# Stage changes of a two-model kernel: weight chunks split ahead of each norm, and a new order of work around them

## The chip, the cores and the metric

One core of one Trainium2 chip. The metric is the device time of one execution in microseconds, the median of several runs. The kernel before took 2974.73 us (three runs, 2971.39 to 2978.29).

## What is computed

Two small transformers run one after the other on 256 tokens of width 1024 (`D`), everything in float32. The first has a short convolution, a SwiGLU, a dilated attention and a mixture of eight experts; the second takes the first one's output and a context of 256 more tokens through a mixer of mLSTM and gated linear attention, a convolutional feed-forward, an RWKV-7 mixer and another such feed-forward. Every one of these layers is wrapped in the same way, and the change is about that wrapping:

```
def modulated_residual(x, c, g, w_mod, b_mod, fn):
    shift, scale, gate = ada_params(c, w_mod, b_mod)
    h = rms_norm(x, g) * (1 + scale) + shift
    return x + gate * fn(h)          # fn begins with h @ W

hl = modulate(rmsnorm(xl, norm_g[layer, 0]), mod_l[0], mod_l[1])   # second model, latent
hc = modulate(rmsnorm(xc, norm_g[layer, 0]), mod_c[0], mod_c[1])   # second model, context
v  = (hn + (shift(hn) - hn) * mu[3]) @ w_rkv[2]                    # RWKV values, both sequences
```

## The kernel before

Activations are kept transposed, eight blocks (`KT`) of 128 channels, each 256 tokens wide; the second model keeps both sequences side by side in `xj`, sequence 0 the context, 1 the latent. A product in float32 precision is made of three matmuls: each operand is split into a high part (`hi`, rounded by ScalarE) and a low part (`lo`, the rest, by VectorE), and TensorE adds hi·hi, hi·lo and lo·hi. `wchunk` (L239) does it for weights: SyncE loads a chunk of 512 KB into `raw`, ScalarE writes `whi` (L254), VectorE `wlo` (L255). There are three pairs of `whi`/`wlo`, so that a chunk can be split only when the one three before it has been used.

Each call of `wchunk` also gives credit to a background job (`background`, L151), which loads modulation weights for a later layer; `mods_v` sums them on VectorE into `macc` (L211, L213).

Where one layer ends and the next begins, the order is always this. The last products are added into `x`; ScalarE squares, TensorE sums the squares over partitions (L331), ScalarE takes Ln and Exp to get the inverse root; then for each block VectorE multiplies (`nt`), ScalarE adds the shift and rounds (`hh`), VectorE makes the low part (`hl`). That is `modulated` (L359) for one sequence and `modulated2` (L917) for two. The first matmul of the next layer needs the first `hh`, the first `whi`, and soon `hl` and `wlo`.

Six stage changes are touched:

- into the SwiGLU (layer 0), about 150 us from the start; into the attention (`layer1_attn`), about 356 us, where after the norm the positions are loaded (L500) and cast by VectorE (L502) for the rotary tables;
- out of the experts into the second model's first mixer, about 1370 us. `first_norms` (L1411) makes the first model's final norm and the second model's first norm from one pass of squares, then calls `modulated2` for both sequences, then scales `x` eight times (L1441). Then come the mixer's masks (`masks0`, L882), then `even_mixer` (L972) with the narrow gate weights (raw loads L981, split L300 and L301, 24 matmuls L990) and the wide ones (L293);
- into the feed-forward `conv_ffn2`, about 1715 us, with background jobs for the next layer at 48 steps over 66 chunks;
- into the RWKV projections (`rwkv_project`, L1524), about 2112 us: `mix(3)` (L1551) norms, shifts and mixes all eight blocks, then the value product (L1590) runs over two halves of 512 output columns (`c`), and inside over pairs of blocks (`k0`), with four banks of PSUM;
- into the last feed-forward `conv_ffn1`, about 2747 us.

Each engine and each queue works its instructions strictly in the order in which they were put there when the program was built. That order isn't the order of the program text: a planner with a timing model of its own walks along, and whenever an engine is free in its model it takes, of the instructions that the model holds ready, the one that stands first in the text. Moving a call ahead in the text therefore gives it precedence and does not of itself make it run earlier.

Of the kernel before, what the change touches and what calls it, by code (L numbers as in the profile page):

```python
# [14 lines left out]
P = 128  # L15
# [17 lines left out]
def _body(es, tc, A, out, upto, dbg):  # L33
# [106 lines left out]
    back.update(jobs=[], rate=0.0, credit=0.0)  # L140
# [10 lines left out]
    def background(jobs, chunks):  # L151

        back["jobs"] += [g for _, g in jobs]
        back["rate"] = sum(n for n, _ in jobs) / chunks
        back["credit"] = 0.0
# [285 lines left out]
    def layer0():  # L441
# [39 lines left out]
        a01 = scale_col("a01", NG(0, 1), m01[:, 8:16])  # L481
        hh, hl = modulated(fb, x, a01, m01[:, 0:8], st=st.rstd())
# [7 lines left out]
    def layer1_attn():  # L490
# [5 lines left out]
        a10 = scale_col("a10", NG(1, 0), m10[:, 8:16])  # L496
        hh, hl = modulated(fb, x, a10, m10[:, 0:8], st=M.get("rs"))
# [384 lines left out]
    def masks0(pl):  # L882
# [17 lines left out]
        nc.vector.memset(reset, 1.0)  # L900
        rv = reset.rearrange("p z (c u) -> p z c u", u=64)
        nc.vector.memset(rv[:, 0, :, 0:1], 0.0)
        nc.vector.memset(rv[:, 1, :, 63:64], 0.0)
# [68 lines left out]
    def even_mixer(pl, xs, y):  # L972

        W = A["ev_w_in_2"][0]
        ML_CN, ML_M0, GL_S = H0["CN"], H0["M0"], H0["S"]

# [5 lines left out]
        whi = whl.tile([P, 1024], F32R, name="whi")  # L982
        wlo = whl.tile([P, 1024], F32R, name="wlo")
        split(raw[:, :896], whi[:, :896], wlo[:, :896])
        hi, lo = (t[:, :896].rearrange("p (k n) -> p k n", k=8) for t in (whi, wlo))
# [22 lines left out]
        with ExitStack() as st:  # L1008
# [402 lines left out]
    def first_norms(pl, xj, cols):  # L1411

        x = xj[:, :, 1]
        if "fin" not in stages:
            return modulated2(pl, xj, cols, seqs(rstd2(xj)))
# [3 lines left out]
        nc.vector.tensor_tensor(ga, fg, cols[1][0], op=MULT)  # L1419

        pt = ps.tile([P, 512], F32, name="st")
# [20 lines left out]
        return xs  # L1442

    def layer2_0(xj):
# [16 lines left out]
        with phase("m0", dict(mm=4, tr=2, sc=2, st="sc"), t2=5), ExitStack() as st:  # L1461
# [6 lines left out]
            even_mixer(pl, xs, y)  # L1468
# [52 lines left out]
    def rwkv_project(pr, pl, xj, cols):  # L1521
# [29 lines left out]
        def mix(i, both=True, first=False):  # L1551
# [3 lines left out]
            for k in range(KT):  # L1555
# [24 lines left out]
        xs = mix(3, first=True)  # L1580
        V = o["V"] = pr.tile([P, 2, 2, D], F32, name="V")
        for c in range(2):
            pts = [ps.tile([P, 512], F32, name="mm") for _ in range(4)]
            for k0 in range(0, KT, 2):
                hi, lo = wchunk(rkv[2][k0 * P:(k0 + 2) * P, c * 512:(c + 1) * 512].rearrange("(k p) n -> p k n", p=P), [2, 512])
                for i in range(4):
                    for k in range(2):
                        xh, xl = (t[:, i * P:(i + 1) * P] for t in xs[k0 + k])
                        for j, (w, x_) in enumerate(((hi, xh), (hi, xl), (lo, xh))):
                            nc.tensor.matmul(pts[i], x_, w[:, k], start=(k0 + k + j == 0), stop=(k0 + k == 7 and j == 2))  # L1590
            for i in range(4):
                nc.scalar.activation(V[:, i // 2, i % 2, c * 512:(c + 1) * 512], pts[i], AF.Copy)
# [636 lines left out]
    def layer2_1(xj):  # L2229
# [108 lines left out]
```

## Time and profile before

| what | value |
|---|---|
| median of three runs | 2974.73 us (2971.39 to 2978.29) |
| the profiled execution, own time | 2965.52 us |
| its span, first to last instruction | 2963.7 us |
| TensorE busy | 2795.3 us, 94% |
| VectorE busy | 2270.0 us, 77% |
| ScalarE busy | 1700.2 us, 57% |
| mean granted TensorE clock | 0.970 of full |

The profiled execution was 9.2 us shorter than the median of the runs. Busy time of TensorE counts pipelined matmuls, and tells little of whether a stretch is full; the table by stretches of time, the order of instructions on an engine (timeline) with the idle time ahead of each and what ended it, and the chain of waits tell more. In this profile the chain that ended last can be followed back to about 1390 us only; the start of the execution has to be read from timelines.

### The profile page before, as it was taken

The numbers are of one execution on the slowest core, as the hardware profiler recorded it, in microseconds if no ns is written. First come the engines' busy times: TensorE is split into PE (matmuls) and PEld (weight loads), VectorE is DVE, ScalarE is ACT, GpSimd is POOL, SyncE is SP. The second block draws the span as 40 slices with busy tenths as digits, with TensorE's granted clock in tenths as the row PEclk, the third lists the DMA queues.
The fourth block names the chain that finished last, engine by engine and source line by source line (L and its number), as shares of the span: only waits on it lengthen the run. The fifth ranks groups of instructions, "written<-read, shape, count | busy, mean of one in ns | idle before, by whom it ended". The sixth has DMA issues, their size and how long they took to land.

```text
span 2963.7 us, 50177 instructions
## 1 busy us (share of the span) xinstructions
PE 2795.3 (94%) x19215; PEld 2269.2 (77%) x19237; DVE 2270.0 (77%) x3945; ACT 1700.2 (57%) x2897; POOL 16.8 (1%) x96
## 2 busy tenths in 40 slices
PE   7999899899999999997999889999699999999998
PEld 4999876688777877875867668888477777667998
DVE  3999673799898988987666498768767887675886
ACT  3565443677777877875455444333457677564454
POOL 0000000000000000000000000000000000000000
PEclk9999999999999999998999999999899999999999
DMA  9989677799898998994311235554222111113463
GB/s 320 325 285 348 226 220 250 269 349 355 295 376 329 328 338 331 356 318 142 93 36 51 79 105 180 169 172 143 81 76 48 29 30 20 18 27 110 130 185 122
DMA packets 410412, 567.73 MB, mean 192 GB/s; under 512 B 79719, under 2 KB 241715, under 8 KB 410163
## 3 DMA queue, kind: packets, MB, share of 16 engines
q1 hardware_dynamic: 406976, 561.79, 56.0%
q8 instruction: 153, 2.51, 0.3%
q10 hardware_dynamic: 3187, 2.65, 0.3%
q14 instruction: 96, 0.79, 0.1%
HBM read 559.11 MB, written 5.24 MB: 190 GB/s over the span
## 4 chain that ended last, share of the span: by engine, by line
PE 41%; DVE 7%; ACT 3%; DMA 1%; issue 1%; SPq 0%; ACTq 0%; DVEq 0%
PE mm L293 20%; PE mm L958 2%; PE yp L1389 2%; PE mm L1590 1%; PE kc L1697 1%; PE tr L1957 1%; PE p L2014 1%; PE p L1993 1%; PE p L2037 1%; PE mm L1855 1%; PE p L2026 1%; PE mm L1878 1%; PE tr L1944 1%; PE sc L1271 1%; PE tr L1575 0%
## 5 line engine op out<-in xcount | busy, mean ns | idle before, releaser
L254 ACT ACTIVATE whi<-raw 128x1024 fp32r<-128x1024 f32 (+3 forms) x868 | 875.8, 1019 | 597.9 <-PE mm L293 164.8
L255 DVE TENSOR_TENSOR wlo<-raw,whi 128x1024 fp32r<-128x1024 f32 (+3 forms) x868 | 1002.7, 1171 | 196.8 <-ACT whi L254 169.1
L795 PE MATMUL mm<-wlo,XH 128*128 128x512 f32 (+1 forms) x768 | 289.3, 379 | 6.6 <-DVE wlo L255 6.1
L795 PE MATMUL mm<-whi,XL 128*128 128x512 f32 (+1 forms) x768 | 289.9, 378 | 0.0
L293 PE MATMUL mm<-hh,whi 128*128 128x512 f32 (+1 forms) x800 | 280.1, 352 | 10.1 <-DVE fg L1341 3.2
L795 PE MATMUL mm<-whi,XH 128*128 128x512 f32 (+1 forms) x768 | 287.8, 375 | 0.2 <-ACT whi L254 0.2
L293 PE MATMUL mm<-hh,wlo 128*128 128x512 f32 (+1 forms) x800 | 278.0, 348 | 4.6 <-DVE wlo L255 4.6
L293 PE MATMUL mm<-hl,whi 128*128 128x512 f32 (+1 forms) x800 | 278.4, 349 | 0.0
L213 DVE SCALAR_TENSOR_TENSOR macc<-raw,sc,macc 128x512 f32<-128x512 f32 x238 | 175.7, 747 | 30.0 <-DMA raw<-in_w_mod_dram 26.5
L293 PEld LDWEIGHTS mm<-hh,whi 128*128 128x128 f32 x800 | 154.9, 194 | 30.8 <-issue 4.7
L795 PEld LDWEIGHTS mm<-wlo,XH 128*128 128x128 f32 x768 | 145.5, 189 | 36.2 <-DVE wlo L255 10.8
L293 PEld LDWEIGHTS mm<-hh,wlo 128*128 128x128 f32 x800 | 154.5, 193 | 24.0 <-DVE wlo L255 5.0
L293 PEld LDWEIGHTS mm<-hl,whi 128*128 128x128 f32 x800 | 154.6, 193 | 18.7 <-issue 1.0
L795 PEld LDWEIGHTS mm<-whi,XH 128*128 128x128 f32 x768 | 145.5, 190 | 24.5 <-ACT whi L254 0.6
L795 PEld LDWEIGHTS mm<-whi,XL 128*128 128x128 f32 x768 | 145.3, 189 | 24.6
L271 PE MATMUL mm<-hh,whi 128*128 128x256 f32 x544 | 153.7, 283 | 3.9 <-ACT hh L368 3.9
L271 PE MATMUL mm<-hl,whi 128*128 128x256 f32 x544 | 153.1, 282 | 0.2 <-DVE hl L372 0.2
L271 PE MATMUL mm<-hh,wlo 128*128 128x256 f32 x544 | 152.7, 281 | 0.0
L1341 DVE SCALAR_TENSOR_TENSOR fg<-mm,c_fcw,fg 128x189 f32<-128x189 f32 (+2 forms) x352 | 143.9, 426 | 4.6
L813 PE MATMUL mm<-whi,muh 128*128 128x512 f32 x352 | 138.2, 393 | 0.1
L813 PE MATMUL mm<-whi,mul 128*128 128x512 f32 x352 | 137.2, 390 | 0.0
L813 PE MATMUL mm<-wlo,muh 128*128 128x512 f32 x352 | 117.3, 393 | 0.2
(700 smaller groups left out, 5890.1 us busy)
## 6 DMA issues: line engine op xcount, KB each, us to landing
raw<-in_moe_w_down_dram SPq DMA_DIRECT2D x176, 512.0 KB, 7.3
raw<-in_moe_w_gate_dram SPq DMA_DIRECT2D x160, 512.0 KB, 5.2
raw<-in_moe_w_up_dram SPq DMA_DIRECT2D x160, 512.0 KB, 5.4
raw<-in_ffn_w_up_dram SPq DMA_DIRECT2D x110, 512.0 KB, 4.6
raw<-in_mod_w_dram SPq DMA_DIRECT2D x96, 512.0 KB, 5.8
raw<-in_w_mod_dram SPq DMA_DIRECT2D x96, 512.0 KB, 4.5
raw<-in_ffn_w_down_dram SPq DMA_DIRECT2D x62, 512.0 KB, 4.4
raw<-in_ev_w_in_dram SPq DMA_DIRECT2D x28, 512.0 KB, 3.7
```

Of the source, the lines that this page charges most:

```text
L213: nc.vector.scalar_tensor_tensor(acc, w[:, kk], v[:, k + kk:k + kk + 1], acc, op0=OP.mult, op1=OP.add)
L254: nc.scalar.activation(hi[:, :n], raw[:, :n], AF.Copy)
L255: nc.vector.tensor_tensor(lo[:, :n], raw[:, :n], R(hi[:, :n]), op=OP.subtract)
L271: nc.tensor.matmul(pt[:, b], w[:, k, b * P:(b + 1) * P], x[:, k0 + k], start=(k0 + k + b == 0 and j == 0), stop=(k0 + k == kt - 1 and j == ...
L293: nc.tensor.matmul(pts[b], w[:, k, b * P:(b + 1) * P], x_, start=(k0 + k + j == 0 and (b == 0 or N != T)), stop=(k0 + k == kt - 1 and j == ...
L795: nc.tensor.matmul(pt[:, :n], xx[:, k0 + k, i], w[:, k], start=(k0 + k == 0 and j == 0), stop=(k0 + k == 7 and j == 2))
L813: nc.tensor.matmul(py[q], xx[:, k0 + k], w[:, k, q * 512:(q + 1) * 512], start=(k0 + k == 0 and j == 0), stop=(k0 + k == FB - 1 and j == 2))
L958: nc.tensor.matmul(pts[i][:, :n], x_, w[:, k], start=(k0 + k + j == 0), stop=(k0 + k == 7 and j == 2))
L1271: nc.tensor.matmul(o, l, r, start=(n == 0), stop=(n == len(jobs) - 1), skip_group_check=True)
L1341: nc.vector.scalar_tensor_tensor(d4[:, ro, co], s4[:, ri, cin], tap(dy, dx), d4[:, ro, co], op0=MULT, op1=ADD)
L1389: nc.tensor.matmul(yk[k], w[:, 0, k * P:(k + 1) * P], u, start=(f + b + j == 0 and k % 2 == 0), stop=(f + b == FB - 1 and j == 2 and k % 2 ...
L1590: nc.tensor.matmul(pts[i], x_, w[:, k], start=(k0 + k + j == 0), stop=(k0 + k == 7 and j == 2))
```

## The change

`ready` and `ready4` call `wchunk` for the first two chunks of the next layer ahead of the norm's code and put the split pairs on a list; the next two calls of `wchunk` take them from there. They are called ahead of the SwiGLU, the attention, both convolutional feed-forwards and the RWKV values. Into the second model's first mixer the narrow weights are loaded and split inside `first_norms`; the context's eight products come ahead of the final norm's end, the blocks are then written sequence by sequence, and the scaling of `x` and the masks move behind the mixer's value product. The background jobs of `conv_ffn2` start after ten chunks and then go faster. RWKV's values are mixed two blocks at a time, each pair followed by its share of the product for both halves of the columns, in eight banks of PSUM. Some `memset`s go from VectorE to GpSimd, and a small tile that nobody reads shifts the addresses of the last stage's tiles.

```diff
-    def background(jobs, chunks):
+    def background(jobs, chunks, wait=0):
         back["jobs"] += [g for _, g in jobs]
-        back["rate"] = sum(n for n, _ in jobs) / chunks
-        back["credit"] = 0.0
+        back["rate"] = sum(n for n, _ in jobs) / (chunks - wait)
+        back["credit"] = -wait * back["rate"]
...
     def wchunk(ap, shape):
+        if back["ready"]:
+            return back["ready"].pop(0)
...
+    def ready(*aps):
+        back["ready"] = [wchunk(a.rearrange("(k p) n -> p k n", p=P), [a.shape[0] // P, a.shape[1]]) for a in aps]
+    def ready4(W):
+        ready(W[0:512, 0:256], W[512:1024, 0:256])
...
+        ready4(A["ffn_w_gate"][0])
         hh, hl = modulated(fb, x, a01, m01[:, 0:8], st=st.rstd())
...
+        ready(A["attn_w_qkv"][0][0:256, 0:512], A["attn_w_qkv"][0][256:512, 0:512])
         hh, hl = modulated(fb, x, a10, m10[:, 0:8], st=M.get("rs"))
...
         reset = pl.tile([P, 2, 2 * T], F32, name="reset")
-        nc.vector.memset(reset, 1.0)
+        nc.gpsimd.memset(reset, 1.0)
...
-    def even_mixer(pl, xs, y):
+    def narrow_weights():
         raw = wraw.tile([P, 1024], F32, name="raw")
         nc.gpsimd.memset(raw[:, :896], 0.0)
...
+        def finish():
+            split(raw[:, :896], whi[:, :896], wlo[:, :896])
+        return finish
...
             gemmT(W, 1024, 512, xs, v_emit)
+            later()
             for s in range(2):
                 mlstm(pm, s, qk, vx, IF, y)
...
+        def product(s, k, a, rs):
+            t = ts[k] if s == 0 else tmp.tile([P, T], F32, name="nt", bufs=2)
+            nc.vector.scalar_tensor_tensor(t, xj[:, k, s], a[:, k:k + 1], rs, op0=MULT, op1=MULT)
+            return t
+        def high(s, k, t):
+            nc.scalar.activation(ops[k][0][:, s], t, AF.Identity, bias=cols[s][1][:, k:k + 1])
+        def low(s, k, t):
+            nc.vector.scalar_tensor_tensor(ops[k][1][:, s], t, cols[s][1][:, k:k + 1], R(ops[k][0][:, s]), op0=ADD, op1=SUB)
...
+        for k in range(KT):
+            product(0, k, cols[0][0], rsb[:, 0])
         cp = tmp.tile([P, 2 * T], F32, name="sq2", tag="t2", bufs=sizes["t2"])
         nc.scalar.activation(cp, pt, AF.Copy)
...
+        got = between()
+        for k in range(3):
+            high(0, k, ts[k])
...
         nc.scalar.activation(fr, fr, AF.Exp, scale=-0.5)
-        xs = modulated2(pl, xj, [cols[0], (ga, cols[1][1])], [rsb[:, 0], fr[:, 1]])
-        for k in range(KT):
-            nc.vector.scalar_tensor_tensor(x[:, k], x[:, k], fg[:, k:k + 1], fr[:, 0], op0=MULT, op1=MULT)
+        for k in range(3):
+            low(0, k, ts[k])
+        for k in range(KT + 1):
+            if k < KT:
+                t = product(1, k, ga, fr[:, 1])
+                high(1, k, t)
+                if k >= 3:
+                    high(0, k, ts[k])
+            if last is not None:
+                low(1, k - 1, last)
+            if 3 <= k < KT:
+                low(0, k, ts[k])
+            last = t
+        def scale():
+            for k in range(KT):
+                nc.vector.scalar_tensor_tensor(x[:, k], x[:, k], fg[:, k:k + 1], fr[:, 0], op0=MULT, op1=MULT)
...
-            xs = first_norms(pl, xj, both("a20", 0, 0))
-            masks0(pl)
+            xs, scale, narrow = first_norms(pl, xj, both("a20", 0, 0), narrow_weights())
+            def later():
+                scale()
+                masks0(pl)
...
-                background([j0, j1], 66)
+                background([j0, j1], 66, 10)
+            ready4(A["ffn_w_up_2"][0])
             xs = modulated2(pl, xj, both("a21", 2, 3), rs)
...
-        xs = mix(3, first=True)
+        ready(rkv[2][0:256, 0:512], rkv[2][0:256, 512:1024])
+        xs = []
-        for c in range(2):
-            pts = [ps.tile([P, 512], F32, name="mm") for _ in range(4)]
-            for k0 in range(0, KT, 2):
+        pts = [ps.tile([P, 512], F32, name="tr" if i < 2 else "mm") for i in range(8)]
+        for k0 in range(0, KT, 2):
+            xs += mix(3, first=True, ks=(k0, k0 + 1))
+            for c in range(2):
                 hi, lo = wchunk(rkv[2][k0 * P:(k0 + 2) * P, c * 512:(c + 1) * 512]...)
...
+            pl.tile([P, 48], F32, name="beside")
+            ready4(A["ffn_w_up_2"][1])
             hh, hl = modulated(pl, x, scale_col("a31", NG2(1, 2), m(4)), m(3), bufs=2, st=M["rsr"])
```

## Rows read from the trace of the kernel before

**Rows 1.** The page's first part: busy us, share of the span, instructions.
```profile
PE 2795.3 (94%) x19215; PEld 2269.2 (77%) x19237; DVE 2270.0 (77%) x3945; ACT 1700.2 (57%) x2897; POOL 16.8 (1%) x96
```
**Rows 2.** ScalarE's timeline into the SwiGLU: start, us, operation, idle before and releaser.
```profile
147.73 1.06 ACT L254 ACTIVATE whi<-raw 128x1024 fp32r<-128x1024 f32 x1 [2.19 <-PE mm L271]
```
**Rows 3.** Timeline of ScalarE, then VectorE, into the attention.
```profile
356.10 1.04 ACT L254 ACTIVATE whi<-raw 128x1024 fp32r<-128x1024 f32 x1
357.04 1.29 ACT L368 ACTIVATE hh<-nt,mod_m 128x256 fp32r<-128x256 f32 x3
...
356.22 1.28 DVE L367 SCALAR_TENSOR_TENSOR nt<-xj,a,rs 128x256 f32<-128x256 f32 x3 [1.44 <-ACT rs L349]
...
363.04 0.17 DVE L502 CAST pos<-pos_i 128x2 f32<-128x2 int32 x1 [5.27 <-DMA pos_i<-in_positions_dram]
...
364.27 0.88 DVE L372 SCALAR_TENSOR_TENSOR hl<-nt,mod_m,hh 128x256 fp32r<-128x256 f32 x2
```
**Rows 4.** Stretches into the attention: us, busy by engine, granted clock, DMA share, GB/s.
```profile
365.00:370.00 5.00, 5.00 (x14) 3.75 (x14) 5.00 (x16) 4.07 (x7) 0.00 (x0) 0.61 1.05 397
370.00:375.00 5.00, 4.81 (x20) 2.95 (x20) 5.00 (x11) 1.82 (x3) 0.00 (x0) 1.00 0.83 280
```
**Rows 5.** Chain of waits out of the experts: start, us, piece.
```profile
1394.68 1.01 DVE wlo L301
...
1395.74 7.16 PE tr L990 x22
```
**Rows 6.** TensorE's timeline there.
```profile
1383.26 0.77 PE L990 MATMUL tr<-hh,whi 128*112 128x512 f32 x1 [4.88 <-ACT hh L927]
...
1396.30 0.63 PE L990 MATMUL tr<-hh,whi 128*112 128x512 f32 x1
1396.73 0.63 PE L990 MATMUL tr<-hl,whi 128*112 128x512 f32 x1
```
**Rows 7.** Timelines of VectorE (two lines) and ScalarE (one) there.
```profile
1382.31 1.54 DVE L926 SCALAR_TENSOR_TENSOR nt<-xj,fga,frs 128x256 f32<-128x256 f32 x4
...
1391.29 3.24 DVE L1441 SCALAR_TENSOR_TENSOR xj<-xj,c_a,frs 128x256 f32<-128x256 f32 x8
...
1380.20 0.93 ACT L300 ACTIVATE whi<-raw 128x896 fp32r<-128x896 f32 x1
```
**Rows 8.** Chain of waits in the first feed-forward of the second model.
```profile
1745.12 1.15 DVE wlo L255
...
1746.31 7.19 PE mm L293 x20
...
1782.49 32.66 PE mm L293 x144
```
**Rows 9.** TensorE's timeline at that point.
```profile
1746.31 0.80 PE L293 MATMUL mm<-hh,wlo 128*128 128x512 f32 x1 [4.57 <-DVE wlo L255]
```
**Rows 10.** The background sums (macc) alone, by stretches there: us, VectorE busy.
```profile
1717.00:1742.00 25.00, 5.47 (x8) 0.93 0.20 64
1742.00:1754.00 12.00, 3.54 (x7) 0.72 0.57 172
```
**Rows 11.** All engines over the RWKV mixing: us, PE, PEld, DVE, ACT, POOL, clock.
```profile
2111.00:2139.00 28.00, 10.57 (x28) 7.33 (x27) 25.34 (x52) 16.31 (x30) 0.00 (x0) 0.63 0.52 170
2111.00:2177.00 66.00, 48.57 (x196) 38.79 (x195) 51.58 (x91) 31.10 (x52) 0.00 (x0) 0.84 0.35 108
2177.00:2199.00 22.00, 19.10 (x74) 13.20 (x73) 20.46 (x47) 13.48 (x25) 2.61 (x13) 0.83 0.00 0
```
**Rows 12.** Chain of waits into the RWKV projections.
```profile
2110.55 7.00 DMA raw<-in_rw_w_rkv_dram
...
2132.90 43.92 PE mm L1590 x184
```
**Rows 13.** Timelines there: TensorE's first matmul, then ScalarE.
```profile
2119.20 1.22 PE L1590 MATMUL mm<-whi,mh 128*128 128x512 f32 x2 [7.51 <-ACT mh L300]
...
2113.63 2.10 ACT L1534 ACTIVATE hf<-hf,mod_b1a 128x256 f32<-128x256 f32 x5 [0.55 <-DVE hf L1533]
```

More of the change, by code (lines that the diff above doesn't have):

```diff
@@ L137, in _body @@
     nc.vector.tensor_scalar(msel, mi, 0.0, None, op0=OP.is_equal)
-    back.update(jobs=[], rate=0.0, credit=0.0)
+    back.update(jobs=[], rate=0.0, credit=0.0, ready=[])
     def back_step():
@@ L899, in masks0 @@
         reset = pl.tile([P, 2, 2 * T], F32, name="reset")
-        nc.vector.memset(reset, 1.0)
+        nc.gpsimd.memset(reset, 1.0)
         rv = reset.rearrange("p z (c u) -> p z c u", u=64)
-        nc.vector.memset(rv[:, 0, :, 0:1], 0.0)
-        nc.vector.memset(rv[:, 1, :, 63:64], 0.0)
+        nc.gpsimd.memset(rv[:, 0, :, 0:1], 0.0)
+        nc.gpsimd.memset(rv[:, 1, :, 63:64], 0.0)
         mdir = pl.tile([8, 2], F32, name="mdir")
@@ L970, in _body @@
     f2 = lambda t: t.rearrange("p s t -> p (s t)")
-    def even_mixer(pl, xs, y):
+    def narrow_weights():
         W = A["ev_w_in_2"][0]
-        ML_CN, ML_M0, GL_S = H0["CN"], H0["M0"], H0["S"]
         raw = wraw.tile([P, 1024], F32, name="raw")
@@ L981, in even_mixer @@
             nc.sync.dma_start(rv[:, :, r:r + n], W[:, c:c + n].rearrange("(k p) n -> p k n", p=P))
[L982 to L985, printed above, removed]
+        def finish():
+            whi = whl.tile([P, 1024], F32R, name="whi")
+            wlo = whl.tile([P, 1024], F32R, name="wlo")
+            split(raw[:, :896], whi[:, :896], wlo[:, :896])
+            return tuple(t[:, :896].rearrange("p (k n) -> p k n", k=8) for t in (whi, wlo))
+        return finish
+    def even_mixer(pl, xs, y, narrow, later):
+        W = A["ev_w_in_2"][0]
+        ML_CN, ML_M0, GL_S = H0["CN"], H0["M0"], H0["S"]
+        hi, lo = narrow
         pt = ps.tile([P, 512], F32, name="tr")
@@ L1409, in conv_ffn1, with first_norms @@
         return yk, st.rstd()
-    def first_norms(pl, xj, cols):
+    def first_norms(pl, xj, cols, between):
         x = xj[:, :, 1]
         if "fin" not in stages:
-            return modulated2(pl, xj, cols, seqs(rstd2(xj)))
+            return modulated2(pl, xj, cols, seqs(rstd2(xj))), lambda: None, between()
         fg = C1["final_g"]
@@ L1419, in first_norms @@
         nc.vector.tensor_tensor(ga, fg, cols[1][0], op=MULT)
+        ops = [tuple(pl.tile([P, 2, T], F32R, name=n, bufs=8) for n in ("hh", "hl")) for _ in range(KT)]
+        def product(s, k, a, rs):
[6 more added lines that the diff above has]
+            nc.vector.scalar_tensor_tensor(ops[k][1][:, s], t, cols[s][1][:, k:k + 1], R(ops[k][0][:, s]), op0=ADD, op1=SUB)
+        st_ = ExitStack()
+        pt_ = st_.enter_context(tc.tile_pool(reuse_waits="tile", name="fn", bufs=1))
+        POOLS.append(pt_)
+        ts = [pt_.tile([P, T], F32, name="ct", bufs=KT) for _ in range(KT)]
         pt = ps.tile([P, 512], F32, name="st")
@@ L1438, in first_norms @@
         nc.scalar.activation(fr, fr, AF.Exp, scale=-0.5)
-        xs = modulated2(pl, xj, [cols[0], (ga, cols[1][1])], [rsb[:, 0], fr[:, 1]])
-        for k in range(KT):
-            nc.vector.scalar_tensor_tensor(x[:, k], x[:, k], fg[:, k:k + 1], fr[:, 0], op0=MULT, op1=MULT)
-        return xs
+        for k in range(3):
+            low(0, k, ts[k])
+        last = None
+        for k in range(KT + 1):
[9 more added lines that the diff above has]
+            last = t
+        st_.close()
+        def scale():
+            for k in range(KT):
+                nc.vector.scalar_tensor_tensor(x[:, k], x[:, k], fg[:, k:k + 1], fr[:, 0], op0=MULT, op1=MULT)
+        return [tuple(f2(t) for t in o) for o in ops], scale, got
     def layer2_0(xj):
@@ L1464, in layer2_0 @@
             handover0(pl)
-            xs = first_norms(pl, xj, both("a20", 0, 0))
-            masks0(pl)
+            xs, scale, narrow = first_norms(pl, xj, both("a20", 0, 0), narrow_weights())
+            def later():
+                scale()
+                masks0(pl)
             y = pl.tile([P, 2, 2, 2, 512], F32, name="ey")
-            even_mixer(pl, xs, y)
+            even_mixer(pl, xs, y, narrow, later)
             with ExitStack() as st2:
@@ L1549, in shift, with mix @@
                 nc.vector.tensor_scalar(o[:, :, e], h[:, :, e], -1.0, None, op0=MULT)
-        def mix(i, both=True, first=False):
+        def mix(i, both=True, first=False, ks=None):
             r = []
             n = 2 * T if both else T
-            for k in range(KT):
+            for k in range(KT) if ks is None else ks:
                 if first and k % 2 == 0:
@@ L1589, in rwkv_project @@
                         for j, (w, x_) in enumerate(((hi, xh), (hi, xl), (lo, xh))):
-                            nc.tensor.matmul(pts[i], x_, w[:, k], start=(k0 + k + j == 0), stop=(k0 + k == 7 and j == 2))
+                            nc.tensor.matmul(pts[4 * c + i], x_, w[:, k], start=(k0 + k + j == 0), stop=(k0 + k == 7 and j == 2))
+        for c in range(2):
             for i in range(4):
-                nc.scalar.activation(V[:, i // 2, i % 2, c * 512:(c + 1) * 512], pts[i], AF.Copy)
+                nc.scalar.activation(V[:, i // 2, i % 2, c * 512:(c + 1) * 512], pts[4 * c + i], AF.Copy)
         th = o["th"] = pr.tile([P, 2 * T], F32, name="th")
```

## The prediction

> **What bounds the kernel now.** I read the page's busy times first: TensorE is busy 94% of the span, VectorE 77% [rows 1]. So the kernel is bound by TensorE, nearly all of its 2963.7 us is work that the change leaves as it is, and only stretches in which TensorE stands still can be won. Then I read the chain of waits and TensorE's timeline around each of the six stage changes, looking at the idle time ahead of the first matmuls and at what ended it. Each piece below is one such hole.
>
> Two questions decide each place. Was the first chunk's split late at all? And which engine's queue would the earlier call stand in? Where ScalarE splits a chunk in the middle of the old layer's end, the planner has already drawn it forward, and there `ready` adds nothing. The reader sees this into the SwiGLU [rows 2], where a split stands at 147.73 us, ahead of the norm that follows; the row stands for three places, as `conv_ffn2` and `conv_ffn1` are entered in the same way. What TensorE waits for at these three is the norm's own chain, which stays.
>
> **The change part by part.**
>
> *SwiGLU and last feed-forward: 0.* The tail of the layer before hides the splits. One background step moves ahead of the norm with its load on SyncE; VectorE waits for the norm there anyway. The unread tile moves addresses only. If the cover went, one split would cost 1.06 us on ScalarE; I keep 1 us either way for each.
>
> *Attention: 5.0 us.* Here the split was late, by accident. VectorE finished three `nt` at 357.5, then its queue held the cast of the positions (L502), whose load landed 5.27 us later. Behind it stood `wlo` and the first `hl`, at 364.27 [rows 3]. TensorE waits for that `hl`. After the change, `wlo` of the first two chunks has precedence over the cast. `whi` stands at 356.10 and is done at 357.1, so `wlo` takes VectorE at 357.5, in the slot that the cast had; meanwhile the `hh` become ready, and `hl` has precedence over the cast as well. First `hl`: 357.5 + 1.23 = 358.7 with one `wlo` ahead, 359.9 with two. Won: 364.27 less that, 4.4 to 5.6; I take 5.0. Above: `hl` at once, 357.5, so 6.8. Below: 0, if the planner keeps the cast ahead. It then lands unnoticed behind the `hl`s. The background's load still goes between the first two chunks on SyncE, as before. The stretch after it is full on TensorE [rows 4], so the gain isn't lost to the loads.
>
> *First mixer: 10.0 us.* TensorE starts the narrow matmuls at 1383.26 [rows 6], then waits for the narrow `wlo` (L301), done at 1395.7 [rows 5]. That one stood behind everything on VectorE: all of `modulated2`, the eight scalings (3.24 us from 1391.29) and the masks [rows 7]. After: the scalings, masks and `reset` go behind the value product; the context's products come ahead of the norm's end, into time in which VectorE waited for it. The second sequence's products still start at 1382.31, since they wait for Exp. From there VectorE has 8 products, 8 low parts of the latent and 5 of the context, 21 x 0.39 us (1.54 / 4) = 8.1 us, so the last operands stand at 1390.4. The narrow `whi` is on ScalarE at 1380.20, its `wlo` (1.01 us) goes ahead of the products while Exp runs. TensorE takes 24 x 0.43 = 10.3 us at the low clock (starts 1396.30 and 1396.73 [rows 6]), less if the clock rises midway: it ends at 1391 to 1393.6. Before it ended at 1395.74 + 7.16 = 1402.9. Won 9.3 to 11.9; I take 10.0, towards the end that keeps the low clock. Below: if `whi` (0.93 us) goes ahead of Ln, the narrow `wlo` after the first products, and the first wide `wlo`s (2 x 1.2 us) after all operands, 4.3 us are lost: 6. The scalings and masks, moved behind the value product, and GpSimd's share of them (that engine is busy 16.8 us in all [rows 1]), cost nothing as long as they are done during the wide products; uncovered, they would delay the mLSTM's first scans by the scalings' 3.24 us and some masks, 5 at most. SyncE now issues the narrow loads ahead of the wide ones; before, one wide load went first, and the planner put its split behind the narrow one.
>
> *`conv_ffn2`: 5.0 us.* The chain shows `wlo` at 1745.12 as what releases TensorE [rows 8]; TensorE had stood still for 4.57 us, since 1741.74 [rows 9]. VectorE is full before that, and 5.47 + 3.54 us of its work from 1717 to 1754 are background sums [rows 10]. Those of the first ten chunks disappear from here, so `wlo` can come up to 6 us earlier, ahead of 1741.74. That wins the 4.57 us, and the low clock after it: the 20 matmuls took 7.19 us where 144 take 32.66 (0.227 each), so 7.19 - 4.54 = 2.6, some of it missing records; I count 1.5. Of these 6.1 I take 5.0, as the convolution's own steps still precede that `wlo`; bounds 2 and 6.4. The sums come back later at 48/56 = 0.857 steps a chunk in place of 48/66 = 0.727: the product of the second matrix lies there, with no convolution on VectorE; I cost it at nothing, 2 us if the planner puts them into the next convolutions.
>
> *RWKV values: 8.5 us.* Before: two matmuls at 2119.20 [rows 13], a few more, then stillness until 2132.9, as all eight blocks are mixed first; then 43.92 us of product [rows 12]. VectorE mixed the four pairs in 25.34 us, three `wlo` among them [rows 11], so a pair costs it (25.34 - 3 x 1.2) / 4 = 5.4 us, and 7.8 with its two `wlo`; it feeds 48 matmuls x 0.227 = 10.9 us. TensorE is the slower one, and doesn't stop any more. 192 matmuls from 2119.2, the first 4.3 us at the low clock: 10 x 0.43 + 182 x 0.227 = 45.6, so it ends at 2164.8, 12 ahead of 2176.8. Against it: `ready` puts two splits ahead of all `hf` in precedence, and the first chunk lands only at 2117.55 [rows 12]. Before, ScalarE did five `hf` first, from 2113.63 [rows 13]. Should both splits stand ahead of them, they begin at 2117.55 + 2 x 1.06 = 2119.7, 6 us later, and the first matmul with them; behind them it is nothing. I take 3.5 us, for a place between: 8.5. Bounds 3 (6 us, and 3 more as VectorE's 51.6 us from 2111 to 2177 [rows 11] have to fit into about 57) and 12.
>
> **The sum.** 5.0 + 10.0 + 5.0 + 8.5 = 28.5 us. Against the profiled execution, 2965.5 - 28.5 = 2937.0 (its span 2963.7 and 1.8 around it); that one was 9.2 us shorter than the median of the runs. For the median: 2974.7 - 28.5 = 2946.2.
>
> **The rivals.**
>
> *The planner keeps the order* (the change doesn't do what it says in the attention, and the mixing is held by its first split): 0 + 10 + 5 + 5 = 20, so 2955. For it: three of six places show that precedence in the text moved nothing [rows 2]. Against it: `wlo` is ready when the cast is taken [rows 3].
>
> *VectorE takes over in the RWKV stage.* After the product it was busy 20.46 of 22 us [rows 11]; if its mixing of the other operands slips as the product moves forward, the product ends earlier and the stage doesn't: 8.5 lost, 2955. Against it: buffers of finished pairs come free during the product.
>
> *The low clock stays* (slower). TensorE would be fed piece by piece where it had stood still and then run in one go. If the pauses keep it at 1.2 GHz through the value product, that takes 192 x 0.43 = 82.6 us from 2122.7 and ends at 2205.3, 28.5 after 2176.8; with the 20.0 won elsewhere the whole is 8.5 us slower, 2983. At 0.2 us lost on each, it decides from about 150 of the 192 on. Against it: in the attention, fed by VectorE in the same way, the granted clock was 0.61 in one stretch and 1.00 in the next [rows 4]. The Trainium skill speaks for it ("TensorE: Matmul & The Clock Gate", section "Loop structure matters more than you think": a loop that waits for its data ahead of each group of matmuls runs them cold, one that keeps them back to back stays warm). By that rule the time would be the 2983 only if each pair waited; the rows of VectorE's pace say that it doesn't.
>
> *Most of it given back*: new orders elsewhere cost as much as the holes; 2972.
>
> **How the numbers follow.** Forecast 0.55 (2938 to 2954); the order kept 0.20; VectorE in RWKV 0.12; given back 0.08; low clock 0.05. All parts at their upper bounds, 6.8 + 11.9 + 6.4 + 12 = 37, give 2938; all at the lower, 0 + 6 + 2 + 3 = 11, give 2964; the three runs spread by 3.5 to each side, so the range is 2934 to 2966. It leaves out the last two rivals. About 0.2% (6 us) is what can be told from no change: faster 0.89, same 0.06, slower 0.05.
>
> **What would show it.** In the profile after: `hl` into the attention 5 us after Exp, the cast behind it; the narrow matmuls without a hole of 6.7 us; no stillness of TensorE between the first two pairs of `conv_ffn2`; the value product unbroken from its first matmul. I am wrong if ScalarE or VectorE waits for a weight's load ahead of the norm's steps, if the mLSTM's scans start later against the value product, or if the stage after the value product is longer than 22 us.

## The result, and the profile after

The changed kernel took 2934.57 us in the median of four runs (2931.97 to 2940.43), against 2973.06 us for the kernel before on the same chip: a ratio of 0.9877 with a 95% interval of 0.9858 to 0.9896, or 36.5 us of 2969 (31 to 42). Timed once more later, the ratio was 0.9889 (0.9873 to 0.9904), 33 us. The forecast was 2946, from a sum of 28.5 us; the time lies 11.6 us below it, just inside the lower end of the range.

The two profiled executions differ by less, 2965.52 to 2940.43, 25.1 us. That of after was the longest of its four, and lost some 7 us ahead of the experts that the next profile of the same kernel did not lose (table below). One execution against another can't be read to better than a few microseconds. Most single stages can, as the table's "like before" column shows; where the granted clock differs, a stage can move by 1 to 5 us too.

The page's first part for after, as [rows 1] for before:

```profile
PE 2796.6 (95%) x19237; PEld 2267.2 (77%) x19237; DVE 2265.4 (77%) x3942; ACT 1702.2 (58%) x2897; POOL 17.8 (1%) x99
```

TensorE's work is the same; stillness went. In the changed program `whi` is L256, `wlo` L257, the wide products L303.

**Attention.** VectorE's timeline in after, then two lines of TensorE's (start, us, operation, idle before and releaser); VectorE's before is in [rows 3], and the last line here is TensorE's before:

```profile
357.54 1.28 DVE L377 SCALAR_TENSOR_TENSOR nt<-xj,a,rs 128x256 f32<-128x256 f32 x3 [1.44 <-ACT rs L359]
358.74 1.22 DVE L257 TENSOR_TENSOR wlo<-raw,whi 128x1024 fp32r<-128x1024 f32 x1
359.87 0.87 DVE L382 SCALAR_TENSOR_TENSOR hl<-nt,mod_m,hh 128x256 fp32r<-128x256 f32 x2
...
364.63 0.17 DVE L514 CAST pos<-pos_i 128x2 f32<-128x2 int32 x1 [2.70 <-DMA pos_i<-in_positions_dram]
...
361.90 0.80 PE L592 MATMUL mm<-whi,hl 128*128 128x512 f32 x1
362.50 0.63 PE L592 MATMUL mm<-wlo,hh 128*128 128x512 f32 x1
```

```profile
364.80 0.80 PE L580 MATMUL mm<-whi,hl 128*128 128x512 f32 x1 [5.02 <-DVE hl L372]
```

From the first `nt` to the first `hl` it is 2.3 us, against 8.1 in [rows 3]. The cast still makes VectorE wait, but behind three `hl`; TensorE has operands and goes on. Its wait of 5.02 us for `hl` is gone.

**First mixer.** TensorE's waits from 1372 to 1437 us in after (engine, line, releaser: us in total, times, longest), pieces of its chain of waits, and TensorE's line for the hole in before:

```profile
PE st L1465 <- DVE sq L1463: 4.8, 1, 4.8
PE tr L1010 <- ACT hh L1450: 4.6, 1, 4.6
PE st L1471 <- ACT sq L1469: 0.7, 1, 0.7
...
1384.12 3.55 PE tr L1010 x7
1387.67 0.70 PE mm L303 x2
1388.37 1.39 PE tr L1010 x6
```

```profile
1395.74 0.77 PE L990 MATMUL tr<-hh,wlo 128*112 128x512 f32 x1 [6.69 <-DVE wlo L301]
```

The wait of 4.6 us for `hh` answers to the 4.88 in [rows 6]. The second one of before, 6.69 us for the narrow `wlo` and the reason for [rows 5], is gone.

**`conv_ffn2`.** The chain there in after. In place of [rows 8 and 9] TensorE runs from the first matmul on:

```profile
1711.17 0.04 issue
1711.22 48.95 PE mm L303 x207
```

**RWKV values.** TensorE's first matmul in after, and the stretches (us, busy PE, PEld, DVE, ACT, POOL, clock, DMA), as [rows 13 and 11]:

```profile
2108.32 1.22 PE L1656 MATMUL tr<-whi,mh 128*128 128x512 f32 x2 [6.96 <-ACT mh L310]
...
2108.00:2115.00 7.00, 6.68 (x22) 4.77 (x23) 6.87 (x12) 3.99 (x7) 0.00 (x0) 0.74 0.88 271
2115.00:2120.00 5.00, 5.00 (x24) 4.14 (x23) 5.00 (x9) 3.15 (x6) 0.00 (x0) 1.00 0.72 227
...
2154.00:2176.00 22.00, 17.78 (x74) 11.64 (x73) 20.46 (x47) 13.49 (x25) 2.57 (x12) 0.93 0.00 0
```

The product is unbroken, the clock full after 7 us, and the stage behind it 22 us long as before.

**Stage by stage.** Each row is the time in us between two landmarks in the profiled execution: the starts of the first or last matmul of a line. "Like before" gives the range over the kernels of the next section whose part doesn't touch that stretch. Left out are the entry to the last feed-forward (57.9 before, 56.1 and 54.5 in the two profiles of after) and stretches that differ by less than 2 us.

| stretch | before | like before | one part alone | after | after, 2nd profile |
|---|---|---|---|---|---|
| start to q, k, v | 357.6 | 354.2–358.9 | | 358.9 | 355.0 |
| to the router | 172.8 | 172.4–173.6 | attention 168.1 | 169.6 | 168.3 |
| router to experts | 17.2 | 16.8–18.4 | attention 18.4 | 19.6 | 17.2 |
| experts to final norm | 824.3 | 821.0–825.7 | | 824.4 | 825.5 |
| first narrow matmul to value product | 63.2 | 63.1–63.2 | mixer 53.1 | 52.2 | 52.2 |
| end of mLSTM to end of value product | 114.2 | 114.2–114.3 | mixer 118.9 | 117.0 | 117.0 |
| to the RWKV values (with `conv_ffn2`) | 475.7 | 475.1–476.4 | `conv_ffn2` 470.5 | 472.1 | 473.7 |
| RWKV values and what follows them | 79.1 | 79.1–79.9 | RWKV 67.7 | 67.0 | 67.9 |
| RWKV recurrence | 215.4 | 215.2–218.4 | RWKV 214.1 | 218.0 | 217.3 |
| last feed-forward | 155.9 | 155.9 | tile 151.6 | 151.5 | 152.8 |

### The profile page after: what moved, and what is told of

Read it like the earlier page. It is cut to its first block, busy times and chain, and to the rows that moved or that the text cites. A ratio compares the mean times of both kernels' runs of the same rounds, so it can differ in the third digit from the quotient of the medians.

```text
span 2938.6 us, 50202 instructions
## 1 busy us (share of the span) xinstructions
PE 2796.6 (95%) x19237; PEld 2267.2 (77%) x19237; DVE 2265.4 (77%) x3942; ACT 1702.2 (58%) x2897; POOL 17.8 (1%) x99
## 4 chain that ended last, share of the span: by engine, by line
PE 41%; DVE 7%; ACT 3%; DMA 1%; issue 1%; SPq 0%; POOL 0%; ACTq 0%; DVEq 0%; POOLq 0%
PE mm L303 18%; PE mm L970 3%; PE yp L1410 2%; PE tr L2024 1%; PE kc L1764 1%; PE mm L1656 1%; PE p L2081 1%; PE p L2060 1%; PE p L2104 1%; PE p L2093 1%; PE mm L1922 1%; PE tr L2011 1%; PE mm L1945 1%; PE sc L1292 1%; DVE fg L1362 1%
## 5 line engine op out<-in xcount | busy, mean ns | idle before, releaser
L256 ACT ACTIVATE whi<-raw 128x1024 fp32r<-128x1024 f32 (+3 forms) x868 | 875.7, 1019 | 547.4 <-PE mm L303 153.4
L257 DVE TENSOR_TENSOR wlo<-raw,whi 128x1024 fp32r<-128x1024 f32 (+3 forms) x868 | 1002.4, 1171 | 175.7 <-ACT whi L256 146.1
L303 PE MATMUL mm<-hh,whi 128*128 128x512 f32 (+1 forms) x800 | 276.3, 347 | 8.5 <-DVE fg L1362 3.6
L303 PE MATMUL mm<-hl,whi 128*128 128x512 f32 (+1 forms) x800 | 275.8, 346 | 0.0
L303 PE MATMUL mm<-hh,wlo 128*128 128x512 f32 (+1 forms) x800 | 275.1, 344 | 0.0
L303 PEld LDWEIGHTS mm<-hh,whi 128*128 128x128 f32 x800 | 152.7, 191 | 28.8 <-issue 5.1
L303 PEld LDWEIGHTS mm<-hl,whi 128*128 128x128 f32 x800 | 152.1, 190 | 18.5 <-issue 1.0
L303 PEld LDWEIGHTS mm<-hh,wlo 128*128 128x128 f32 x800 | 151.8, 190 | 18.6 <-issue 1.0
L281 PE MATMUL mm<-hl,whi 128*128 128x256 f32 x544 | 152.8, 281 | 0.0
```

What stands on the lines that cost most here:

```text
L281: nc.tensor.matmul(pt[:, b], w[:, k, b * P:(b + 1) * P], x[:, k0 + k], start=(k0 + k + b == 0 and j == 0), stop=(k0 + k == kt - 1 and j == ...
L303: nc.tensor.matmul(pts[b], w[:, k, b * P:(b + 1) * P], x_, start=(k0 + k + j == 0 and (b == 0 or N != T)), stop=(k0 + k == kt - 1 and j == ...
```

## The experiments

### One part at a time

Five kernels, each the kernel before with one part of the change (and the helpers `ready`, `ready4` and `wait`).

```diff
 only_attn:  +ready(attn_w_qkv[0:256, 0:512], attn_w_qkv[256:512, 0:512])   # ahead of the norm
 only_mixer: +narrow_weights, first_norms(..., between), later()            # and reset on GpSimd
 only_ffn:   -background([j0, j1], 66)  +background([j0, j1], 66, 10)  +ready4(ffn_w_up_2[0])
 only_rwkv:  +mix(3, ks=(k0, k0 + 1)) pair by pair, 8 banks, +ready(...)
 tile_only:  +pl.tile([P, 48], F32, name="beside")  +ready4(...)            # SwiGLU, last feed-forward
```

Attention. 

> The attention's part alone (ready ahead of its norm; all else as before). Forecast step: hl stands 5 us earlier and the experts start 5 us earlier, about 5 us in all (bounds 0 and 6.8). Rival, from the profile of after: the q, k, v and output products end 4 to 5 us earlier, but ScalarE then waits for the router's weights, whose load shares the queues with the experts' first weights, so the experts start at the same time as before and the whole gains 0 to 1 us. A third: the planner's other order of the attention's VectorE work costs something, and the whole is slower by 1 to 3 us.

Mixer. 

> The first mixer's part alone (context's products ahead of the norm's end, narrow weights split between, scalings and masks behind the value product). Forecast step: narrow matmuls end 10 us earlier and the whole is 10 us shorter (bounds 6 and 11.9). Rival, from the profile of after: some 3 us of it are given back at the end of the value product and in the mLSTM (there the lead fell from 10.1 to 7.3 us), so about 7 us in all. If the masks uncovered cost what I bounded, 5 us.

`conv_ffn2`. 

> conv_ffn2's part alone (no background work in the first ten chunks, first chunks split ahead of the norm). Forecast step: the 4.57 us of stillness and most of the low clock after it go, 5 us (bounds 2 and 6.4). Rival one, from the profile of after, where the lead grew by 3.6 us between the mixer's end and the value product of the RWKV layer: 3 to 4 us, as the sums moved back cost 1 to 2 us later in the stage. Rival two: nothing, if the sums then hold the convolutions.

RWKV. 

> The RWKV layer's value product alone (mixed two blocks at a time, first two chunks split ahead). Forecast step: 8.5 us (bounds 3 and 12), with the first split costing 3.5 of 12. Rival, from the profile of after: the first split stood in nobody's way and the product ends 12 us earlier; carried to the end 12 us, or 8 if the recurrence after it gives 4 back, as the lead there fell from 23.0 to 19.1. If VectorE took over after the product: 0 to 2 us.

Tile. 

> Only the entries of the SwiGLU and of the last feed-forward: ready ahead of both norms, and the unread tile of 192 bytes a partition in the last one. All instructions of all engines stand in the order of the kernel before; only addresses in the last feed-forward differ. My forecast for this part: 0 (1 us either way). Rival, from the profiles: between the first and the last feed-forward matmul the kernel before and the three kernels with other parts took 155.8 to 155.9 us, after 151.5, and its 256-column matmuls follow each other at 113 to 118 ns in place of 120; if the tile's shift does that, this kernel shows 151.5 there and is 4 us faster in all.

Measured against the kernel before on the same chip; us are the ratio's distance from 1 on 2969 us, with its interval:

| part | forecast | ratio | us by it |
|---|---|---|---|
| attention | 5.0 | 0.9992 | 2.4 (−1.5 to 5.9) |
| first mixer | 10.0 | 0.9977 | 6.8 (4.2 to 9.5) |
| `conv_ffn2` | 5.0 | 0.9982 | 5.3 (1.8 to 9.2) |
| RWKV values | 8.5 | 0.9957 | 12.8 (8.3 to 17.2) |
| unread tile, `ready4` at two feed-forwards | 0 | 0.9982 | 5.3 (2.1 to 8.6) |
| sum | 28.5 | | 32.6 |
| all, timed twice | | 0.9877, 0.9889 | 36.5, 33.0 |

The parts add up to the whole within their intervals; the attention's alone can't be told from nothing. With `ready4` at the SwiGLU and the last feed-forward (as in the tile's kernel) the built program has the same instructions in the same order on every engine as before, and `conv_ffn2`'s part has one order with and without its `ready4`. At three of six places `ready4` does nothing, as forecast; in `conv_ffn2` all of the gain is the background's ten chunks of rest. TensorE's waits there (1715 to 1800 us), first with the part alone, then before:

```profile
PE mm L303 <- ACT hh L937: 2.9, 1, 2.9
PE st L341 <- ACT sq L333: 1.2, 3, 0.5
```

```profile
PE mm L293 <- DVE wlo L255: 4.6, 1, 4.6
PE mm L293 <- ACT hh L927: 2.9, 1, 2.9
```

Just behind that window stands a new wait, 1.6 to 2.2 us in the five kernels that have the part and in none of the nine without it: TensorE waits for `fuh`, which stands behind a `whi` on ScalarE whose load landed late. With the part alone, ScalarE and TensorE:

```profile
1818.91 1.06 ACT L256 ACTIVATE whi<-raw 128x1024 fp32r<-128x1024 f32 x1 [3.53 <-DMA raw<-in_ffn_w_down_dram]
...
1820.54 0.50 PE L303 MATMUL mm<-fuh,whi 128*128 128x512 f32 x1 [1.73 <-ACT fuh L310]
```

### RWKV: what do the pairs do, and what does `ready`?

```diff
 pairs_noready: the RWKV part without
-        ready(rkv[2][0:256, 0:512], rkv[2][0:256, 512:1024])
 rwkv_ready: the kernel before with
+        ready(rkv[2][0:256, 0:512], rkv[2][256:512, 0:512])
         xs = mix(3, first=True)
```

> The RWKV part without ready: mixed two blocks at a time, first chunks drawn where the product asks for them. If ready's early load and split are what lets TensorE start at once, this is 1 to 4 us slower than the RWKV part with it (12.8 us by the ratio); by the step of my forecast, where the first splits stand ahead of the norm's steps and cost 3.5 us, it is 3.5 us faster; if ready is idle here, the same.

> The RWKV part the other way round: ready alone (the first two chunks of the first column half split ahead), the mixing in one piece as before. My forecast's step said that TensorE stood still because all eight blocks are mixed first, and that ready costs something; by it this kernel is no faster (0, or 3 us slower). Rival, after the run with pairs and without ready gained nothing and its longest wait was 9.9 us for wlo: it is the low part of the first chunk, behind the mixing in VectorE's queue, that holds TensorE. Then ready alone takes the stillness away, the value product goes from 57.2 to 46 to 50 us and the whole is 8 to 12 us faster.

Measured: pairs without `ready` 1.0001 (0.9988 to 1.0014), nothing gained, and the product took 57.3 us, 57.2 before. `ready` without pairs 0.9958 (0.9945 to 0.9971), by the ratio all of the gain; the product took 47.5 us, with both 45.9. TensorE's waits from 2105 to 2180 us, of before, of the pairs alone, and of `ready` alone:

```profile
PE mm L1590 <- DVE wlo L255: 9.9, 1, 9.9
PE mm L1590 <- ACT mh L300: 7.5, 1, 7.5
```

```profile
PE mm L1600 <- DVE wlo L257: 9.9, 1, 9.9
PE mm L1600 <- ACT mh L310: 7.3, 1, 7.3
```

```profile
PE mm L1601 <- ACT mh L310: 7.2, 1, 7.2
...
PE mm L1601 <- DVE wlo L257: 1.2, 1, 1.2
```

The stillness was a wait for one `wlo`, which the planner had put behind the mixing on VectorE. Breaking the mixing into pairs left that `wlo` where it was; asking for it ahead of the norm moved it. The mixing itself kept up with TensorE without pairs, but for 1.2 us of waiting for a `wlo`; with `ready` there, the pairs are worth some 1.6 us of the product (one profile of each), less than the ratio can show.

### The mixer: the narrow weights, or the masks and scalings?

```diff
 mixer_masks_first: the mixer's part with
+            scale()
+            masks0(pl)
+            later = lambda: None
```

> The first mixer's part with one piece put back: the scalings and the masks stand ahead of the mixer's products again, the context's products and the narrow weights stay early. The first wide low parts then stand behind some scalings and the masks on VectorE. If the narrow weights' place alone made the gain, the stretch from the first narrow matmul to the first matmul of the value product stays at 53 us (63 before). If the scalings and masks held TensorE as well, by what stands ahead of the wide wlo (eight scalings of 0.4 us and eight small mask operations), it is 55 to 58 us.

Measured: 0.9993 (0.9983 to 1.0002), against 0.9977 for the whole part. The stretch to the value product was 59.9 us, longer than either side expected. TensorE's waits from 1375 to 1445 us:

```profile
PE tr L1008 <- ACT hh L1448: 5.2, 1, 5.2
PE mm L303 <- DVE wlo L257: 3.5, 1, 3.5
PE mm L303 <- ACT whi L256: 0.9, 1, 0.9
```

So the early narrow weights and context's products alone win some 3 of the 10 us. With masks and scalings ahead, the next `wlo` in the queue, a wide one, is late, 3.5 us; the hole moves by one product.

### Addresses alone

```diff
 addr_only: the kernel before with
+            pl.tile([P, 32], F32, name="shift")       # first mixer, 128 bytes
+                po.tile([P, 16], F32, name="shift_o") # its output product, 64 bytes
+            pl.tile([P, 16], F32, name="beside")      # last feed-forward, 64 bytes
+            # and both ready4 of the tile's kernel, which leave every order as it was
```

> The kernel before with nothing but addresses changed (same instructions in the same order): the unread tile in the last feed-forward is 64 bytes in place of 192, and in the first mixer two unread tiles move the latent's and the heads' operands from 128 and 64 bytes past a multiple of 256 to a multiple of 256, where the operands of conv_ffn2 lie. If the pace of matmuls hangs on where the moving operand lies against the weights: the last feed-forward runs at 113 to 118 ns a matmul, not 120 (4 to 9 us won), and the mixer's 512-column matmuls at 226 to 227 ns as in conv_ffn2, not at 229 to 232 (about 670 of them, 3 us won). If it was something else in after: no change.

Measured: 0.9985 (0.9972 to 0.9999). The last feed-forward took 153.0 us (155.9 before; with 192 bytes 151.5, 151.6 and 151.6 in three profiles, 152.8 and 152.9 in two others). In the mixer, from the first narrow matmul to the value product 62.1 in place of 63.2, and 0.6 us less in the next stretch: 1.6 us of the 3 expected. But then the stretch after the mLSTM took 116.0 us in place of 114.2, by the clock (last section). Groups of the last feed-forward (line, engine, operation, tiles, count; busy us, mean ns), of the kernel before and of the tile's kernel:

```profile
L293 PE MATMUL mm<-hh,wlo 128*128 128x256 f32 x257 | 72.7, 283 | 0.0
...
L293 PEld LDWEIGHTS mm<-hh,wlo 128*128 128x128 f32 x256 | 49.2, 192 | 0.0
```

```profile
L303 PE MATMUL mm<-hh,wlo 128*128 128x256 f32 x257 | 71.9, 280 | 0.0
...
L303 PEld LDWEIGHTS mm<-hh,wlo 128*128 128x128 f32 x256 | 48.1, 188 | 0.0
```

Stretches of 20 us there, before, with the tile, and in the second profile of after, which has the same tile: TensorE is full in all of them, but with 169 matmuls before, 179, then 172, with the tile alone, and 172 from the start in the last:

```profile
2810.00:2830.00 20.00, 20.00 (x169) 20.00 (x168) 17.45 (x34) 9.89 (x15) 0.00 (x0) 1.00 0.60 182
```

```profile
2801.00:2821.00 20.00, 20.00 (x179) 20.00 (x178) 18.40 (x34) 10.57 (x16) 0.00 (x0) 1.00 0.65 201
2821.00:2841.00 20.00, 20.00 (x172) 20.00 (x171) 18.41 (x32) 10.66 (x15) 0.00 (x0) 1.00 0.64 202
```

```profile
2775.00:2795.00 20.00, 20.00 (x172) 20.00 (x171) 17.93 (x33) 10.90 (x17) 0.00 (x0) 1.00 0.63 200
```

### The router's weights, and a version that beats both

```diff
 after_rw: the changed kernel with, in layer1_attn,
+        rw = M["rw"] = const.tile([P, 8, 8], F32, name="rw")
+        nc.scalar.dma_start(rw, A["router_w"][0].rearrange("(k p) e -> p k e", p=P))
         pos_i = fb.tile([P, 2], I32, name="pos_i")
 after_rw_addr: after_rw with the two tiles of addr_only in the first mixer
 after_again: the changed kernel as it is
```

> The changed kernel with the router's weights loaded at the start of the attention, in place of after the norm ahead of the experts; the rest as in after. If the attention's gain is given back because ScalarE waits for that load among the experts' first weights (4.86 us in after), the router's matmuls come some 4 us earlier after the norm and the experts start 4 us earlier: 4 us faster than after. If something else holds the experts' start (their own first weights, the top-k's chain), the wait goes and the start stays: 0 to 1 us.

> The changed kernel once more, to stand beside the next one on the same chip. By the ratio measured first, 36 us below the kernel before; by the sum of the single parts (0.8 + 2.3 + 1.8 + 4.3 + 1.8 thousandths for the unread tile), 33 us. If the parts do not add up, it lies outside 30 to 40.

> The changed kernel with the router's weights loaded early, and with the first mixer's operands moved to a multiple of 256 bytes by unread tiles. Expected 4 to 7 us below the changed kernel for the router's weights (in the one profile so far the stretch from the first attention product to the router's first matmul was 6.8 us shorter), and 1 to 2 us for the addresses. If the experts' start is bound by their own weights, 1 to 2 us in all.

Measured: after_rw 2931.41 us, ratio 0.9873 (0.9852 to 0.9893); in a later set, side by side, after_again 2935.91 us, 0.9889 (0.9873 to 0.9904), and after_rw_addr 2926.86 us, 0.9856 (0.9839 to 0.9872): 9 us below the changed kernel. By its ratio, after_rw alone can't be told from the changed kernel. ScalarE's wait for the router's weights ahead of the experts, and TensorE's for their split, in the first profile of after; then TensorE's waits for that split and for `hh` in after_rw:

```profile
ACT rwh L310 <- DMA rw<-in_router_w_dram: 4.9, 1, 4.9
...
PE tr L699 <- ACT rwh L310: 7.3, 1, 7.3
```

```profile
PE tr L700 <- DVE rwl L311: 1.4, 1, 1.4
PE tr L700 <- ACT hh L378: 1.4, 1, 1.4
```

From the first attention product to the router it takes 4.8 to 5.6 us less than in the second profile of after (162.8 and 163.6 us in place of 168.3), and 1.6 to 1.8 are given back before the experts (18.8 and 19.0 in place of 17.2). So the load did cost, 3 to 4 us net in the profiles. ScalarE had waited for it in the kernel before as well, 3.0 us: this is a further gain, not the attention's gain restored. Not all of the 9 us comes from the two edits as they were meant: 3.6 us of the distance between the profiles of after_again and after_rw_addr lie in the stretch of `conv_ffn2`, which neither edit touches, and there the clock was higher (below).

## Why the prediction was right, and where it was not

**Attention: mechanism right, end wrong.** `hl` came ahead of the cast, TensorE went on, and the router came 4.7 us sooner after the first product. I said that it "isn't lost to the loads", looking only at the stretch right behind it [rows 4]. Between router and experts 1.2 us are lost with the part alone, 2.3 in the first profile of after, none in the second, and 1.2 also in two kernels that don't touch this place. It isn't a load that takes them. That stretch before, with the attention's part, and with `conv_ffn2`'s, which leaves this place as it was (columns as above):

```profile
530.30:547.70 17.40, 14.05 (x81) 9.65 (x82) 12.89 (x58) 10.65 (x21) 0.00 (x0) 0.79 0.74 286
```

```profile
525.40:543.90 18.50, 15.64 (x81) 11.46 (x82) 12.97 (x58) 10.84 (x20) 0.00 (x0) 0.68 0.64 227
```

```profile
532.00:550.50 18.50, 15.66 (x81) 11.46 (x82) 12.96 (x58) 10.82 (x20) 0.00 (x0) 0.68 0.69 267
```

The same 81 matmuls keep TensorE busy 1.6 us longer at a granted clock of 0.68 in place of 0.79; in the first profile of after it was 0.67, in the second 0.79. By the ratio 2.4 us remain of the forecast's 5.0, with an interval that takes in both 0 and 5.

**Mixer: the hole right, what follows missed.** 63.2 to 53.1 us is the forecast's 10.0, and the chain ends as worked out, with 7 us less of waiting for the narrow `wlo`. But the stretch behind the mLSTM gave back 4.6 us with the part alone, and 2.8 to 4.7 in every kernel that has it. I had bounded a loss there through scalings and masks, "5 at most"; TensorE waits for none of these. Its clock is lower there, 0.91 in place of 0.96 over the stretch, which the forecast didn't price.

**`conv_ffn2`: right in size, with a loss that was costed at nothing.** 5.2 us in the profile and 5.3 by the ratio, for 5.0. The 4.57 us and the low clock after them went, and 1.7 us came back as the wait for `fuh` shown above; whether the background's later loads hold that chunk back was not tried. In the two profiles of after the stretch shows 3.5 and 2.0 us of the gain, in the two kernels with the router's weights early some 5.7. The difference is the clock: TensorE stands still for 29.1 and 29.8 us of the stretch in after, 29.7 with the part alone, 32.1 before; but the same matmuls keep it busy for 443.0 and 443.9 us, against 440.8 with the part alone and 440.8 and 440.9 with the router's weights early. So the clock decides what of the gain shows.

**RWKV: right stretch, wrong reason, too small.** I read the stillness as "all eight blocks are mixed first", and then took 3.5 us off for `ready`. The waits of before name the releaser, the `wlo`: 9.9 us. I had the row of the product's start [rows 12], but not the line ahead of it in the same chain, which is that `wlo`. So `ready` makes the gain and the pairs nearly none of it, as the two kernels showed. The first split, at 2106.7 us in after, waited 1.3 us for its load and delayed nothing: TensorE's wait for the first operand was 6.96 us, 7.51 before. The term that I took off had no ground, and the gain was the upper bound of 12 (11.4 us in the stage with the part alone, 12.8 by the ratio), not 8.5. It is also the place where "`ready` gives precedence" mattered most, and the one where I priced it as a cost.

**Last feed-forward: "the unread tile moves addresses only" was true, and addresses cost.** 0 forecast, 4.3 us measured in the stage, of which only some 3 come in every execution (last section).

**The rivals.** In the attention the planner did not keep the order. VectorE didn't take over: 20.46 us of 22 after the product, the same as in [rows 11]. The low clock did not stay in the value product: 0.74 in its first 7 us, 1.00 after. The rule behind that rival (the Trainium skill, "TensorE: Matmul & The Clock Gate", section "Loop structure matters more than you think") speaks of a loop that waits ahead of each group; here no group after the first waited. The clock did matter, at places where I had no rival: behind the mLSTM, and ahead of the experts. "Most of it given back" had a part in it: new orders did cost elsewhere, 2.8 to 4.7 us behind the mLSTM by the clock and about 1.7 in `conv_ffn2` by a wait, but not as much as the holes.

**The sum.** By the ratios of the parts it is 32.6 in place of 28.5: RWKV +4.3, tile +5.3, `conv_ffn2` +0.3, mixer −3.2, attention −2.6. That the sum came so near is in part luck: terms that were too low and too high, and one that I had at 0, nearly cancel. Most of the rest of the distance to 2946 is the time that I started from: the median of three runs was 2974.7, that of 23 to 30 runs of the kernel before, timed later, 2968.8 to 2969.9, 5 to 6 us less. The profiled execution's own time, 2965.5, was a little nearer to it than the median that I preferred. The range's upper end should by its own terms have been 2967, not 2966.

## What to carry to other kernels

When TensorE stands still, read the releaser in the table of waits before giving the stillness a reason, and follow the small operand (a weight's low part) as well as the large one: three of the four holes were one `wlo` behind other work in VectorE's queue, and the cure was its place in the order, not a finer loop. Then follow the gain on to the next load and the next stage: a stage that starts earlier meets loads that don't, and TensorE's clock there can differ by as much as the gain. If TensorE's busy time changes while its matmuls don't, look at the granted clock before looking for a wait. If matmuls run back to back and still slower than elsewhere in the same kernel, compare where their operands lie.

## What the runs showed of the hardware

**The pace of back-to-back matmuls hangs on an address, and not on that alone.** In the last feed-forward, with the moving operand at a multiple of 256 bytes as the weights are, 256-column matmuls started every 120 ns (median of starts), in all eight profiles of kernels that leave it there. Moved by 64 or 192 bytes they started every 118 ns through most of the stage, and the weight loads took 188 to 191 ns in place of 192. Instructions and order were the same. In three of the five profiles with 192 bytes the pace was 113 ns for the first 30 to 40 us; the first profile of after has that and the second, the same program, does not, so this is no matter of the address alone. What decides it wasn't settled, nor which addresses are best. For 512 columns it was the other way about: a matmul took 395 ns in the mean at 128 bytes past a multiple, 389 at a multiple (the mixer's groups, before and addr_only). The Trainium skill ("SBUF — State Buffer", section "Who interferes with whom") gives the moving operand and the weight load read ports of their own and says that TensorE waits for nobody. These matmuls waited for no other engine in the trace either, and yet their pace differs by 2% (120 against 118 ns) with the operand's address.

**The clock takes a little more or less for the same stillness, and the same program repeats it.** Stretches behind the mLSTM, of before and of the mixer's part (columns as above, the clock ahead of the DMA's share):

```profile
1529.00:1539.00 10.00, 6.18 (x26) 4.79 (x26) 5.25 (x22) 5.33 (x16) 0.00 (x0) 0.69 0.18 52
1539.00:1549.00 10.00, 10.00 (x34) 6.37 (x32) 3.15 (x6) 5.52 (x9) 0.00 (x0) 0.79 0.01 2
...
1569.00:1579.00 10.00, 9.69 (x137) 7.61 (x135) 7.18 (x24) 6.41 (x19) 1.48 (x1) 1.00 0.37 107
```

```profile
1517.00:1527.00 10.00, 6.18 (x26) 5.18 (x26) 4.72 (x20) 4.82 (x15) 0.00 (x0) 0.67 0.18 52
1527.00:1537.00 10.00, 10.00 (x28) 5.99 (x27) 3.05 (x8) 4.47 (x9) 0.00 (x0) 0.65 0.01 2
...
1557.00:1567.00 10.00, 9.86 (x104) 8.18 (x104) 7.16 (x20) 4.46 (x7) 1.81 (x1) 0.66 0.36 107
```

TensorE's busy time is the same (6.18 of 10 us, then 10.00), and so are its waits; but it stays at 1.2 GHz longer, and falls to it a second time 40 us later, where before it ran at 2.4. The stretch took 114.2 or 114.3 us in before and the six kernels that leave the mixer as it was, 117.0 in both profiles of after, and 118.8 or 118.9 in four kernels with the mixer's part; the granted clock over it was 0.96 in before, 0.93 in after and 0.91 with the mixer's part alone. It isn't the order of instructions alone: addr_only, with the order of before and a mixer 1.6 us shorter, took 116.0, at 0.93. What in the time ahead decides it was not tried.
